# A planner's prices for TensorE products, turned blocks as plain products, and small work kept together by the array's tile size

## The chip, the core and the metric

The kernel runs on one core of a Trainium2 chip. Measured is the time of one launch on the device in microseconds (us), as the median of several runs. TensorE (PE in the profile) multiplies, VectorE (DVE), ScalarE (ACT) and GpSimd (POOL) work on rows of 128 partitions, and SyncE (SP) issues most DMA transfers. Each engine works through its own instructions in the order in which the program gives them and waits on semaphores for the others.

## What is computed

The reference is one inference step of two decoder layers in fp32 for 256 prompt rows and 8 sample rows, which share all weights. Layer 0 mixes by RWKV-7 (16 heads of 64) and S5 side by side, layer 1 by retention (8 heads, states of 256x512), and each is followed by a SwiGLU feed-forward block.

```python
for i in range(DEPTH):
    h = rmsnorm(x, norm_mix[i])
    if i % 2 == 0:
        proj = h @ w_in_a[j]                                  # 2048 x 4352
        o_rwkv, sh, S = rwkv7_mix(proj[..., :RWKV_PROJ], ...)
        o_s5, hr, hi = s5_mix(proj[..., RWKV_PROJ:], ...)
        mix = jnp.concatenate([o_rwkv, o_s5], -1) @ w_out_a[j]
    else:
        proj = h @ w_in_c[j]                                  # 2048 x 12288
        mix, S = retention_mix(proj, st_ret[j], pos, ret_gn[j], w_out_c[j])
    x = x + mix.astype(x.dtype)
    h = rmsnorm(x, norm_ffn[i])
    x = x + swiglu(h, ffn_w_gate[i], ffn_w_up[i], ffn_w_down[i]).astype(x.dtype)
```

```python
def step(S, inp):                                             # RWKV-7, one row
    r_t, w_t, k_t, v_t, kk_t, a_t = inp
    sa = jnp.einsum('bhij,bhj->bhi', S, kk_t)
    S = (S * w_t[:, :, None, :] - sa[..., None] * (kk_t * a_t)[:, :, None, :]
         + v_t[..., None] * k_t[:, :, None, :])
    return S, jnp.einsum('bhij,bhj->bhi', S, r_t)
```

## The kernel before

**The stream.** All 264 rows (256 + 8) are held transposed, and the large products run as one stream over the weights. A weight tile of 128x512 (`raw`) is split into a high part `wh` by ScalarE and a low part `wl` by VectorE, and each 128x128 block makes three matmuls with 264 columns in the type float32r: `wh` with `xh`, `wh` with `xl`, `wl` with `xh` (other names of the right-hand side are `hh`, `hl`, `n`, `omh`). So one granule of 12 stream matmuls needs one `wh` and one `wl`; `run_stream` splits two granules ahead. There are 21408 stream matmuls.

**The side work.** Everything between the large products is written as generators: `front`, `back` and `post` for the RWKV-7 heads in pairs `p` of 0 to 7 (prompt rows, in chunks of 64), `rwkv_sample` for the 8 sample rows, `s5` and `s5_out`, and in layer 1 `ret_mix` and `ret_sample`. Their operations are recorded and not issued at once. After every second k-tile, that is after every six stream matmuls, `run_stream` calls `pump`, which issues what is ready by the planner's own clocks: `clk` has one clock for each of TensorE ("P"), VectorE ("V"), ScalarE ("S"), GpSimd ("G") and the DMA ("D"), `cost` gives the price of an operation, `after` the time at which its operands are there, and `emit` moves the clock on and writes the instruction. The order so found is fixed in the program. All instructions of side work and stream are written by the same `getattr` in `emit`, so that the profile shows nearly everything as L279; the names of the tiles tell the work apart.

**Four places that matter below.** (1) `turned(out, a, one)` turns a 64x64 block by a product with `id2`, two identities of 64 below each other. It is called 8 times a pair in `front` and 22 times in `back` (8 + 6 + 8, by `heads`), for the two halves of the partitions by turns. Where the output begins at partition 0 it is a `transpose`, otherwise a plain `matmul`. (2) The S5 recurrence in `s5` has 64 steps on VectorE:

```python
for c in range(64):
    h, o = H[:, :, :, c], H[:, :, :, c + 1]
    self.mul(t, bc(h[:, None], [128, 2, 2, 32]), w)
    self.add(o, o, t[:, 0])
    self.add(o, o, t[:, 1, ::-1])
    if c % 4 == 3:
        yield
```

(3) `rwkv_sample_half` does, for each of 8 head pairs, a product with `bones` (ones in two blocks of 64), a multiply on VectorE, a subtraction on GpSimd, two DMAs which broadcast a row of `srow` into the tile `t` (in the profile `ar_tmp<-ar_tmp`), and then `self.mul(t, t, vb("k"))` on VectorE, a 128x512 multiply that needs them. (4) `ret_sample` in layer 1 updates the states of 8 sample rows a head in two groups `g` of 4: eight multiplies `stt` of 128x512 on VectorE, products with the new states on TensorE, and then `load(1)`, four DMAs of 512 KB from GpSimd's queue into the same four buffers, before the second group.

Of the kernel before, what the change touches and what calls it, by code (L numbers as in the profile page):

```python
# [10 lines left out]
F32R = mybir.dt.float32r  # L11
# [9 lines left out]
T = TP + TS  # L21
# [18 lines left out]
PART = 2, 2  # L40
LOOK = 2, 1
FAR = 1 << 20
ORDER = (("u", 0), ("u", 4), ("q", 0), ("q", 1), ("q", 2), ("q", 3))
LAG = 0.13, 0.2
PS5, PSO, PR = 0, 0, 0
# [14 lines left out]
class Task:  # L60
    def __init__(self, w, row0, nk, c0, rhs, done, need=None):
        self.w, self.row0, self.nk, self.c0 = w, row0, nk, c0
        self.rhs, self.done, self.need, self.pre = rhs, done, need, None
# [64 lines left out]
class Builder:  # L128
    def __init__(self, ctx, tc, ins, outs, dumps=None):
        self.ctx, self.tc, self.nc = ctx, tc, tc.nc  # L130
        self.I, self.O, self.C0 = ins, outs, ins["cst"]
        self.dumps = dumps or {}
        self.side, self.rec = [], None
        self.evac = Side(None, -1)
        self.clk = dict.fromkeys("PVSGD", 0.0)
        self.where, self.uses, self.pend = {}, {}, {}
        self.tick, self.cols, self.warm = 0, 0.0, False
        self.flags = Flags(self)
        self.act_set = None
        nc = self.nc  # L140
        self.V, self.G, self.S, self.P = (Eng(self, e, k) for e, k in
                                          ((nc.vector, "V"), (nc.gpsimd, "G"), (nc.scalar, "S"), (nc.tensor, "P")))
        self.Q, self.QG, self.QS = (Eng(self, e, "D") for e in (nc.sync, nc.gpsimd, nc.scalar))
        pool = lambda name, **k: ctx.enter_context(tc.tile_pool(name=name, **k))
        self.pw = pool("pw", bufs=1)
        self.pc = pool("pc", bufs=1)
        self.pb = pool("pb", bufs=1)
        self.ps = pool("ps", bufs=1, space=PSUM)
        ctx.enter_context(tc.manual_schedule())
        self.banks = [self.ps.tile([128, 512], F32, name=f"ps{i}", tag=f"ps{i}") for i in range(8)]  # L150
        self.layer, self.held = 0, {}
        self.turn, self.bank, self.open, self.busy = 0, {}, [], [None] * 4
        for b in self.banks:
            self.cells(b)


    def psum(self):
# [3 lines left out]
        self.open.append(b)  # L161
        return bass.AP(self.banks[0].tensor, self.turn * FAR, self.banks[0].ap)

    def real(self, x):

        if not hasattr(x, "ap") or not isinstance(x.offset, int) or x.offset < FAR or str(x.space) != str(PSUM):
            return x
        b = self.bank[x.offset // FAR]
        if b.at is None:
            free = [i for i in range(4) if not self.busy[i]]  # L170
            b.at = min(free, key=lambda i: self.uses[self.banks[i].tensor.name].max())
            self.busy[b.at] = b
        return bass.AP(self.banks[b.at].tensor, x.offset % FAR, x.ap)

# [25 lines left out]
    def operands(self, name, a, k):  # L200
# [3 lines left out]
        for i, x in enumerate(aps):  # L204
            if type(x.tensor).__name__ == "Tile":
                if str(x.space) == str(PSUM):
                    far = x.offset // FAR
                    out.append((far or x.tensor.name, self.cells(self.banks[0]), True))
# [4 lines left out]
    def cost(self, key, name, a):  # L213

        n = int(np.prod(a[0].shape[1:])) if hasattr(a[0], "shape") else 1
        if key == "P":
            w = a[2] if name == "transpose" else a[1]
            w = int(np.prod(w.shape[1:]))
            if a[1].dtype == F32R:
                return 0.113 * n / T  # L220
            if name == "transpose":
                return 0.11 if w > 64 else 0.04
            if w <= 32:
                return max(0.034, 0.02 + 0.42e-3 * n)
            if w <= 64:
                return max(0.08, 1.05e-3 * n)
            return max(0.205, 1.68e-3 * n)
        if key == "V":
            fast = name in ("tensor_scalar", "tensor_copy", "memset") and not any(str(x.space) == str(PSUM) for x in a if hasattr(x, "space"))
            c = 0.07 + n * (0.52e-3 if fast else 1.04e-3) + (0.006 * n if name == "reciprocal" else 0)  # L230
            if name.startswith(("tensor_scalar", "scalar")) and any(hasattr(x, "shape") and tuple(x.shape[1:]) == (1,) for x in a[2:]):
                c += 0.07
            return c
        if key == "S":
            return 0.094 + n * 0.83e-3
        if key == "D":
            return 0.03 + n * a[0].shape[0] * 1.11e-5
        return 0.035 + n * 0.83e-3 if name == "memset" else 0.15 + n * 2.05e-3

    def after(self, key, uses):  # L240

        t = 0.0
        for name, (at, bits), w in uses:
            if isinstance(name, int):
                b = self.bank[name].at
                if b is None:
                    name = min((self.banks[i].tensor.name for i in range(4) if not self.busy[i]), key=lambda n: self.uses[n].max())
                else:
                    name = self.banks[b].tensor.name
            u = self.uses[name]  # L250
            for q in (0, 1) if w else (0,):
                for e, k in enumerate("PVSG"):
                    v = u[q, e][at].max()
                    if v:
                        t = max(t, v + (LAG["P" in (k, key)] if k != key else 0.0 if key == "P" or q else 0.125))
        return t

    def emit(self, eng, name, a, k):

        a = [self.real(x) for x in a]  # L260
        key, uses = eng.key, self.operands(name, a, k)
        c = self.cost(key, name, a)
        t = self.after(key, uses)
        if key == "D":
            t = self.clk["D"] = max(t + 1.7, self.clk["D"]) + c
        else:
            if key == "P":
                while self.clk["P"] + 0.1 >= (self.tick + 1) * 3.4133:
                    self.warm = self.cols >= 3277
                    self.tick, self.cols = self.tick + 1, 0.0  # L270
                n = int(np.prod(a[0].shape[1:]))
                self.cols += n * (1 if a[1].dtype == F32R else 2 if name == "transpose" else 4) * a[1].shape[0] / 128
                c *= 1 if self.warm else 2
            elif key == "S":
                self.functions(ACT_SET.get(a[2]))
            t = self.clk[key] = max(self.clk[key], t) + c
        for n, (at, bits), w in uses:
            self.uses[n][0 if w else 1, "PVSG".index(key) if key != "D" else 3][at] = t
        getattr(eng.eng, name)(*a, **k)  # L279
        return t  # L280
# [119 lines left out]

    def turned(self, out, a, one):

        if out.offset % FAR < out.ap[0][0]:
            self.P.transpose(out, a, one)
        else:
            self.P.matmul(out, a, one, start=True, stop=True)

    def gcopy(self, out, a):
        self.G.tensor_scalar(out, a, 1.0, None, op0=OP.mult)
# [90 lines left out]
    def choices(self):  # L500

        for s in self.side + [self.evac]:
            for op in s.ops:
# [12 lines left out]
                        best = t + c, t, i  # L516
                yield best[1], s.pri, op, best[2]

    def pump(self, most):

        left = most
        while True:
            self.refill()
            now = self.clk["P"]
            other, tens = [], []
            for c in self.choices():
                if c[2].keys[c[3]] == "P":
                    if left > 0 and c[2].ready[0] <= now:
                        tens.append((c[1], c[2].ready[0], c))
                elif c[0] <= now:  # L530
                    other.append((c[0], c[1], c))
            if other:
                c = min(other, key=lambda o: o[:2])[2]
            elif tens:
                c = min(tens, key=lambda o: o[:2])[2]
            else:
                return
            t = self.clk["P"]
            self.go(c[2], c[3])
            left -= self.clk["P"] - t  # L540
# [260 lines left out]
    def in_a_tasks(self):  # L801
# [4 lines left out]
        def quad(q):  # L806
            for j in range(3):
                for e in range(2):
                    tile = 8 * j + 2 * q + e
                    n = 3 * (2 * q + e) + j  # L810
                    need = (("free",) + divmod(n - RING, 3),) if n >= RING else ("ush2",) if n >= RING - 5 else ("ush",) if n >= RING - 9 else None
                    ts.append(Task(w, 0, KT, tile * 128, rx, lambda a, t=tile: self.in_a_done(a, t), need))

        def us(t0):
            for t in range(t0, t0 + 4):
                ts.append(Task(w, 0, KT, PROJ + t * 128, rx, lambda a, t=t: self.s5_in(a, t)))

        for f, i in ORDER:
            quad(i) if f == "q" else us(i)
# [989 lines left out]
```

## Time and profile before

| | before |
|---|---|
| median of 3 runs (least, most) | 3212.47 us (3202.04, 3217.61) |
| profiled execution, its own time | 3204.68 us |
| its span | 3202.9 us |
| TensorE busy | 3121.3 us, 97% |
| VectorE busy | 1972.0 us, 62% |
| ScalarE busy | 1498.7 us, 47% |
| GpSimd busy | 343.4 us, 11% |
| DMA moved | 560.54 MB, 175 GB/s on average |

Busy time is the time in which an engine has at least one instruction under way; on TensorE successive matmuls overlap, so their single durations add up to more than that. The granted clock (PEclk) is TensorE's clock as a share of its full 2.4 GHz. In the views, `ps` is a PSUM bank, `ar_tmp`, `ar_hida`, `ar_hidb` and `ar_hidy` are large tiles out of which the side work cuts its own, `cst` holds constants (`id2`, `bones`, `ident`), and `t` with `ar_tmp` is the S5 recurrence.

### The profile page before, as it was taken

The page shows a single profiled execution, that of the slowest core. Times are in us where ns is not written, and L with a number is a line of the kernel's source. Part 1 is how long each engine was busy: PE and PEld are TensorE (multiplying, and loading weights), DVE is VectorE, ACT ScalarE, POOL GpSimd, SP SyncE. Part 2 cuts the span into 40 slices and gives each one's busy share as a digit, 9 for nine tenths or more (in the row PEclk, how much of TensorE's full clock was granted, in tenths as well). Part 3 has the DMA queues.
Part 4 walks back from the last instruction along what each step waited for, and adds up shares of the span by engine and source line. Part 5 has one row for each costly group of instructions (what it writes and reads, how often), then busy time and mean ns, then how long its engine had stood idle before and what let it go on. Part 6 is the DMA issues. An engine that isn't in the chain of part 4 may idle for free.

```text
span 3202.9 us, 65844 instructions
## 1 busy us (share of the span) xinstructions
PE 3121.3 (97%) x26390; PEld 2967.3 (93%) x26390; DVE 1972.0 (62%) x3702; ACT 1498.7 (47%) x2733; POOL 343.4 (11%) x525
## 2 busy tenths in 40 slices
PE   7999798899999999999999999999999999999998
PEld 7987687799999999999998998988899999999998
DVE  6788666466555555566566666565566565555554
ACT  6543355255444444455344444444455444444454
POOL 5111332100000000001111111011100000000001
PEclk9999899799999999999999999999999999999999
DMA  5323413455655556666666677567666555565654
GB/s 192 120 86 74 61 54 70 84 163 183 179 184 180 182 179 184 181 182 211 216 230 219 230 250 254 174 244 250 217 179 184 181 182 184 178 183 180 184 179 152
DMA packets 161138, 560.54 MB, mean 175 GB/s; under 512 B 21312, under 2 KB 23744, under 8 KB 160576
## 3 DMA queue, kind: packets, MB, share of 16 engines
q1 hardware_dynamic: 140384, 483.29, 50.7%
q0 software_dynamic: 19584, 71.31, 5.9%
q8 instruction: 207, 3.39, 0.4%
q10 hardware_dynamic: 864, 1.74, 0.1%
q14 instruction: 99, 0.81, 0.1%
HBM read 511.45 MB, written 42.69 MB: 173 GB/s over the span
## 4 chain that ended last, share of the span: by engine, by line
PE 92%; DVE 3%; DMA 2%; ACT 1%; POOL 1%; issue 0%; SPq 0%; DVEq 0%; POOLq 0%; ACTq 0%
PE ps L279 92%; DMA ar_tmp<-ar_tmp 2%; DVE ar_tmp L279 1%; POOL ar_tmp L279 1%; DVE wl L279 1%; DVE t L279 1%; ACT ar_tmp L279 0%; ACT wh L279 0%; DVE ar_hidb L279 0%; DVE ar_hidy L279 0%; SPq L279 0%; DVE xl L279 0%; DVE ar_hida L279 0%; POOL ar_hida L279 0%; ACT L285 0%
## 5 line engine op out<-in xcount | busy, mean ns | idle before, releaser
L279 DVE TENSOR_TENSOR wl<-raw,wh 128x512 fp32r<-128x512 f32 x1784 | 1260.6, 710 | 904.1 <-ACT wh L279 892.5
L279 ACT ACTIVATE wh<-raw 128x512 fp32r<-128x512 f32 x1784 | 1098.9, 628 | 936.3 <-PE ps L279 905.5
L279 PE MATMUL ps<-xh,wh 128*128 128x264 f32 x4512 | 1330.0, 295 | 14.7 <-ACT wh L279 12.4
L279 PE MATMUL ps<-xh,wl 128*128 128x264 f32 x4512 | 1289.7, 286 | 10.8 <-DVE wl L279 10.7
L279 PE MATMUL ps<-xl,wh 128*128 128x264 f32 x4512 | 1287.8, 285 | 0.0
L279 PEld LDWEIGHTS ps<-xh,wh 128*128 128x128 f32 x4512 | 858.8, 190 | 63.4 <-issue 28.6
L279 PEld LDWEIGHTS ps<-xh,wl 128*128 128x128 f32 x4512 | 856.4, 190 | 12.6 <-DVE wl L279 12.6
L279 PEld LDWEIGHTS ps<-xl,wh 128*128 128x128 f32 x4512 | 860.0, 191 | 5.7 <-issue 4.8
L279 PE MATMUL ps<-hl,wh 128*128 128x264 f32 x1280 | 364.0, 284 | 0.0
L279 PE MATMUL ps<-hh,wl 128*128 128x264 f32 x1280 | 363.9, 284 | 0.0
L279 PE MATMUL ps<-hh,wh 128*128 128x264 f32 x1280 | 363.8, 284 | 0.0
L279 PE MATMUL ps<-n,wh 128*128 128x264 f32 x1408 | 257.4, 284 | 0.0
L279 PE MATMUL ps<-ar_tmp 64*64 64x64 f32 (+8 forms) x2912 | 215.3, 283 | 39.5 <-DVE ar_tmp L279 24.6
L279 PEld LDWEIGHTS ps<-hh,wh 128*128 128x128 f32 x1280 | 241.4, 189 | 0.0
L279 PEld LDWEIGHTS ps<-hl,wh 128*128 128x128 f32 x1280 | 240.9, 188 | 0.0
L279 PEld LDWEIGHTS ps<-hh,wl 128*128 128x128 f32 x1280 | 240.7, 188 | 0.0
L279 PEld LDWEIGHTS ps<-ar_tmp 64*64 64x64 f32 (+3 forms) x2912 | 149.3, 149 | 82.3 <-DVE ar_tmp L279 28.9
L279 POOL TENSOR_TENSOR sqs<-sq,sqs 128x264 f32<-128x264 f32 x56 | 42.4, 758 | 1663.5 <-ACT sq L279 1663.5
L279 PEld LDWEIGHTS ps<-n,wh 128*128 128x128 f32 x1408 | 217.8, 188 | 0.0
L279 PE MATMUL ps<-n,wl 128*128 128x264 f32 x704 | 199.6, 284 | 0.0
L279 PE MATMUL ps<-omh,wh 128*128 128x264 f32 x512 | 147.1, 287 | 0.0
L279 PE MATMUL ps<-omh,wl 128*128 128x264 f32 x512 | 145.6, 284 | 0.0
(214 smaller groups left out, 2872.1 us busy)
## 6 DMA issues: line engine op xcount, KB each, us to landing
raw<-in_w_in_c_dram SPq DMA_DIRECT2D x192, 512.0 KB, 4.3
raw<-in_ffn_w_gate_dram SPq DMA_DIRECT2D x176, 512.0 KB, 3.6
raw<-in_ffn_w_up_dram SPq DMA_DIRECT2D x176, 512.0 KB, 3.7
raw<-in_ffn_w_down_dram SPq DMA_DIRECT2D x176, 512.0 KB, 3.7
out_dram<-ar_tmp POOLq DMA_DIRECT2D x72, 512.0 KB, 4.3
raw<-in_w_in_a_dram SPq DMA_DIRECT2D x68, 512.0 KB, 3.7
ar_tmp<-in_state_ret_dram POOLq DMA_DIRECT2D x64, 512.0 KB, 6.9
raw<-in_w_out_c_dram SPq DMA_DIRECT2D x64, 512.0 KB, 3.8
```

The lines of the kernel that those rows point to most:

```text
L279: getattr(eng.eng, name)(*a, **k)
```

## The change

It has four parts. `cost` prices a product by its weight load (0.004 us and 0.833 ns a column) or its columns, whichever is more, and twice that for fp32. `turned` always writes a plain `matmul`. A new function `tile_of` gives the tile size of the array that a product needs (32, 64 or 128 rows and columns; float32r and transposes count as 128 columns) and its place, and `emit` keeps a clock for each place: products of one size at different places run side by side, and a change of size waits for all and costs 0.09 us and a load more. In `pump`, of the products with the same priority those of the array's present size go first; if all that are ready have another size, `pump` returns, until the oldest has been ready for 2.5 us (`PATIENCE`) or they come to 1.2 us of cost (`TOGETHER`).

```diff
+PATIENCE = 2.5, 2.5
+TOGETHER = 1.2, 1.2
...
@@ cost
+            load = 0.004 + 0.833e-3 * w
             if a[1].dtype == F32R:
-                return 0.113 * n / T
+                return max(load, 0.005 + 0.44e-3 * n)
             if name == "transpose":
-                return 0.11 if w > 64 else 0.04
-            if w <= 32:
-                return max(0.034, 0.02 + 0.42e-3 * n)
-            if w <= 64:
-                return max(0.08, 1.05e-3 * n)
-            return max(0.205, 1.68e-3 * n)
+                return max(load, 0.42e-3 * n)
+            return 2 * max(load, 0.002 + 0.833e-3 * n)
...
+    def tile_of(self, name, a):
+
+        r = lambda n: 32 if n <= 32 else 64 if n <= 64 else 128
+        w = a[1]
+        m = 128 if name == "transpose" or w.dtype == F32R else r(int(np.prod(w.shape[1:])))
+        size = r(int(w.shape[0])), m
+        return size, (w.offset // w.ap[0][0], a[0].offset % FAR // a[0].ap[0][0])
...
@@ emit
                 c *= 1 if self.warm else 2
+                size, at = self.tile_of(name, a)
+                t0 = max(self.clk["P"], t)
+                if size != self.size:
+                    t0 = max([t0, *self.tiles.values()]) + 0.09 + 0.833e-3 * size[1]
+                    self.size, self.tiles = size, {}
+                t0 = max(t0, self.tiles.get(at, 0.0))
+                t = self.tiles[at] = t0 + c
+                self.clk["P"] = t if size == (128, 128) else t0 + 0.012
             elif key == "S":
                 self.functions(ACT_SET.get(a[2]))
-            t = self.clk[key] = max(self.clk[key], t) + c
+            if key != "P":
+                t = self.clk[key] = max(self.clk[key], t) + c
...
     def turned(self, out, a, one):
 
-        if out.offset % FAR < out.ap[0][0]:
-            self.P.transpose(out, a, one)
-        else:
-            self.P.matmul(out, a, one, start=True, stop=True)
+        self.P.matmul(out, a, one, start=True, stop=True)
...
@@ pump
                 if c[2].keys[c[3]] == "P":
                     if left > 0 and c[2].ready[0] <= now:
-                        tens.append((c[1], c[2].ready[0], c))
+                        tens.append((c[1], self.size_of(c[2]) != self.size, c[2].ready[0], c))
...
             elif tens:
-                c = min(tens, key=lambda o: o[:2])[2]
+                if not went and all(o[1] for o in tens) and now - min(o[2] for o in tens) < PATIENCE[self.layer]:
+                    if sum(self.cost("P", *x[1:3]) for o in tens for x in o[3][2].calls[0]) < TOGETHER[self.layer]:
+                        return
+                c = min(tens, key=lambda o: o[:3])[3]
+                went = True
```

Since the planner's clocks differ, the whole order of the side work in the stream differs. Two places on VectorE show it. The first is in the part of layer 0 in which the S5 recurrence runs (`t_77<-t_77,ar_tmp` are its adds, `ar_tmp<-t_77,ar_tmp` its multiply, `wl` the split that the stream needs next, the other rows belong to `front` and `back` of the head pairs). Before, eight successive rows there were:

```order
L279 TENSOR_TENSOR wl<-raw,wh 128x512
L279 TENSOR_TENSOR t_77<-t_77,ar_tmp 128x64
L279 TENSOR_TENSOR ar_hidb<-ar_hidy,ar_hida 64x4x64
L279 TENSOR_TENSOR t_77<-t_77,ar_tmp 128x64
L279 TENSOR_TENSOR ar_tmp<-ar_tmp,ps_70 128x256
L279 TENSOR_TENSOR wl<-raw,wh 128x512
L279 TENSOR_TENSOR ar_tmp<-t_77,ar_tmp 128x128
L279 TENSOR_TENSOR ar_tmp<-ps_71,cst 128x256
```

With the change, a stretch between two `wl` in the same part reads (shown without its last rows):

```order
L296 TENSOR_TENSOR wl<-raw,wh 128x512
L296 TENSOR_TENSOR ar_tmp<-t_77,ar_tmp 128x128
L296 TENSOR_TENSOR ar_tmp<-ps_70,cst 128x256
L296 TENSOR_TENSOR t_77<-t_77,ar_tmp 128x64 x2
L296 TENSOR_TENSOR ar_tmp<-t_77,ar_tmp 128x128
L296 TENSOR_TENSOR t_77<-t_77,ar_tmp 128x64
L296 SCALAR_TENSOR_TENSOR ar_tmp<-ps_69,cst 128x256
L296 TENSOR_TENSOR t_77<-t_77,ar_tmp 128x64
L296 TENSOR_TENSOR ar_tmp<-t_77,ar_tmp 128x128
L296 TENSOR_TENSOR ar_tmp<-ps_71,cst 128x256
L296 TENSOR_TENSOR t_77<-t_77,ar_tmp 128x64 x2
L296 TENSOR_TENSOR ar_tmp<-t_77,ar_tmp 128x128
```

Five steps of the recurrence now stand between two `wl` here (two more adds, one more multiply and one more add follow until the next `wl`), where two adds stand between the two `wl` of the rows before.

The second place is in `ret_sample` of layer 1, at the border between the two groups of states of the first head (`SCALAR_TENSOR_TENSOR ar_tmp<-ar_tmp,ps_..` are the state multiplies; behind the last one of the first group, the second such row of each piece, the four buffers are loaded anew). Before:

```order
L279 SCALAR_TENSOR_TENSOR ar_tmp<-ar_tmp,ps_69 128x512
L279 TENSOR_TENSOR wl<-raw,wh 128x512
L279 SCALAR_TENSOR_TENSOR ar_tmp<-ar_tmp,ps_70 128x512
L279 TENSOR_TENSOR wl<-raw,wh 128x512 x6
L279 TENSOR_TENSOR ar_tmp<-ps_75,rstd 128x264
L279 TENSOR_TENSOR wl<-raw,wh 128x512
L279 TENSOR_TENSOR ar_tmp<-ps_76,rstd 128x264
L279 SCALAR_TENSOR_TENSOR ar_tmp<-ar_tmp,ps_71 128x512
```

With the change:

```order
L296 SCALAR_TENSOR_TENSOR ar_tmp<-ar_tmp,ps_71 128x512
L296 SCALAR_TENSOR_TENSOR ar_tmp<-ar_tmp,ps_72 128x512
L296 TENSOR_TENSOR wl<-raw,wh 128x512 x4
L296 SCALAR_TENSOR_TENSOR ar_tmp<-ar_tmp,ps_69 128x512
L296 SCALAR_TENSOR_TENSOR ar_tmp<-ar_tmp,ps_70 128x512
```

Four `wl` instead of seven stand between the last state multiply of the first group and the first of the second, and the multiplies come in twos.

## Rows read from the trace of the kernel before

**Rows 1.** The page: busy time of each engine, and granted clock in 40 slices.
```profile
PE 3121.3 (97%) x26390; PEld 2967.3 (93%) x26390; DVE 1972.0 (62%) x3702; ACT 1498.7 (47%) x2733; POOL 343.4 (11%) x525
PEclk9999899799999999999999999999999999999999
```
**Rows 2.** Stretches: us, busy PE, PEld, DVE, ACT, POOL, then clock, DMA share, GB/s.
```profile
300.00:400.00 100.00, 79.30 (x789) 64.92 (x789) 61.54 (x147) 28.75 (x81) 35.08 (x55) 0.80 0.43 62
500.00:600.00 100.00, 81.46 (x898) 66.09 (x896) 58.59 (x136) 33.66 (x69) 21.07 (x24) 0.84 0.42 69
700.00:1400.00 700.00, 699.83 (x5770) 699.56 (x5769) 410.37 (x700) 338.23 (x598) 8.67 (x12) 1.00 0.60 182
```
**Rows 3.** What TensorE waited for: us in total, times, longest.
```profile
PE ps L279 <- DVE ar_tmp L279: 28.6, 13, 7.3
PE ps L279 <- ACT wh L279: 12.4, 2, 8.6
PE ps L279 <- DVE wl L279: 10.7, 6, 3.9
```
**Rows 4.** What VectorE waited for in the first 700 us.
```profile
DVE ar_tmp L279 <- DMA ar_tmp<-ar_tmp: 50.0, 8, 9.1
```
**Rows 5.** Timeline of VectorE, a multiply after its broadcast: start, us, instruction, [idle before].
```profile
303.18 0.69 DVE L279 TENSOR_TENSOR ar_tmp<-ar_tmp 128x512 f32<-128x512 f32 x1 [5.95 <-DMA ar_tmp<-ar_tmp]
303.79 0.27 DVE L279 TENSOR_TENSOR t<-t,ar_tmp 128x64 f32<-128x64 f32 x1
303.97 0.41 DVE L279 TENSOR_TENSOR ar_tmp<-ar_tmp,ps 128x256 f32<-128x256 f32 x1
```
**Rows 6.** Timeline of TensorE behind that multiply.
```profile
304.43 1.12 PE L279 MATMUL ps<-ar_tmp 64*64 64x64 f32 x16 [5.19 <-DVE ar_tmp L279]
```
**Rows 7.** Timeline of TensorE: groups of 64x64 products between stream matmuls.
```profile
235.32 1.15 PE L279 MATMUL ps<-ar_tmp 64*64 64x64 f32 x32
...
364.23 0.68 PE L279 MATMUL ps<-ar_tmp 64*64 64x64 f32 x16
...
479.49 1.78 PE L279 MATMUL ps<-cst,ar_tmp 64*64 64x64 f32 x12
```
**Rows 8.** Groups of TensorE instructions by shape, the turned blocks: busy us, mean ns, idle before.
```profile
L279 PE MATMUL ps<-cst,ar_tmp 64*64 64x64 f32 x192 | 30.6, 256 | 0.1
...
L279 PE MATMUL ps<-cst,ar_hida 64*64 64x64 f32 x75 | 11.3, 243 | 0.0
...
L279 PE MATMUL ps<-cst,ar_hidb 64*64 64x64 f32 x45 | 7.4, 260 | 1.3 <-DVE ar_tmp L279 1.3
...
L279 PE MATMUL ps<-cst,t 64*64 64x64 f32 x48 | 7.1, 243 | 0.0
```
**Rows 9.** Groups of VectorE instructions by shape, 100 to 700 us.
```profile
L279 DVE TENSOR_TENSOR wl<-raw,wh 128x512 fp32r<-128x512 f32 x150 | 113.0, 757 | 41.5 <-ACT wh L279 40.5
L279 DVE TENSOR_TENSOR t<-t,ar_tmp 128x64 f32<-128x64 f32 x128 | 40.3, 315 | 1.2
L279 DVE TENSOR_TENSOR ar_tmp<-ar_tmp,ps 128x256 f32<-128x256 f32 x72 | 29.3, 414 | 11.2 <-PE ps L279 10.6
L279 DVE TENSOR_TENSOR ar_tmp<-t,ar_tmp 128x128 f32<-128x128 f32 x64 | 27.1, 424 | 0.5
```
**Rows 10.** Timelines of TensorE, GpSimd and VectorE in layer 1, a reload of states.
```profile
1578.33 0.39 PE L279 MATMUL ps<-xh,wh 128*128 128x264 f32 x1
...
1578.67 1.58 POOL L279 DMA_DIRECT2D ar_tmp<-in_state_ret_dram  x3 [2.01 <-PE ps L279]
...
1588.47 0.69 DVE L279 SCALAR_TENSOR_TENSOR ar_tmp<-ar_tmp,ps 128x512 f32<-128x512 f32 x1 [1.43 <-PE ps L279]
```
**Rows 11.** The tile of the retention states: its 64 loads, from issue to landing.
```profile
DMA to landing us min/median/max: 3.8/6.9/12.5
```
**Rows 12.** Two stretches with turned blocks, columns as in the stretches above.
```profile
192.00:199.00 7.00, 7.00 (x49) 5.10 (x48) 5.03 (x13) 2.74 (x6) 3.18 (x7) 0.74 0.05 4
482.00:485.40 3.40, 3.40 (x36) 2.92 (x34) 2.24 (x6) 2.87 (x4) 1.35 (x4) 0.51 0.73 246
```

More of the change, by code (lines that the diff above doesn't have):

```diff
@@ L137, in __init__ @@
         self.tick, self.cols, self.warm = 0, 0.0, False
+        self.size, self.tiles = None, {}
         self.flags = Flags(self)
@@ L517, in choices, with size_of @@
                 yield best[1], s.pri, op, best[2]
+    def size_of(self, op):
+        return self.tile_of(*op.calls[0][0][1:3])[0]
     def pump(self, most):
-        left = most
+        left, went = most, False
         while True:
```

## The prediction

> **What bounds the kernel now.** I read the page first. TensorE is busy 97% of the span, mostly at the full clock level [rows 1]: it sets the time, so a microsecond counts only if TensorE works less, waits less or runs at the higher clock for longer. The view of stretches shows where anything is left to win. From 700 us on, TensorE does 5770 stream matmuls in 699.83 us, 0.1213 us each, at granted clock 1.00; before that, slices of 100 us fall to 79.30 and 81.46 us busy at clocks of 0.80 and 0.84 [rows 2]. Layer 0's small work lies there. The waits of TensorE name what is late: VectorE's `ar_tmp` above all, 28.6 us in 13 waits, then ScalarE's `wh` and VectorE's `wl` [rows 3]. Largely they go back to one thing: VectorE sits idle 50.0 us, eight times, until a DMA has brought the broadcast row of the sample state [rows 4]. Its multiply at 303.18 stood 5.95 us for that [rows 5], and TensorE's next product 5.19 us behind it [rows 6].
>
> **The turned blocks.** `turned` is called 240 times (8 head pairs of 8 in `front` and 22 in `back`); 120 were transposes, by turns with plain products. A plain fp32 product is two rows in the trace, a transpose one. A group of 12 rows (4 transposes, 4 products) takes 1.78 us, a group of 8 plain products (16 rows) 0.68 us [rows 7]: 1.10 less per 8, and 30 eights make 33. Check from the other side: all 360 rows of this kind are busy 30.6 + 11.3 + 7.4 + 7.1 = 56.4 us [rows 8]; 30 x 0.68 is 20.4, so 36 less. I take 33 and keep 36 as the bound. The other bound: if such a block gained only by a shared switch, 0. The rows leave no doubt that the alternation is what costs, since 16 rows are shorter than 12.
>
> The Trainium skill has a sentence the other way: "TensorE: Matmul & The Clock Gate", section Terms, says of the weight load and the matmul that their transpose mode is four times faster for FP32. By that the 120 turned blocks would lose: a plain one is 0.68 / 8 = 0.085 us [rows 7], a quarter of that 0.021, and 120 x 0.064 would be 7.7 us more. The trace does not agree in this setting.
>
> **The list by tile size.** It should merge groups of small products. Counted through both orders, it hardly does: changes of tile size other than those of the transposes go from 555 to 540, and the groups of small work between stream matmuls from 159 to 172 in layer 0 (155 to 163 in layer 1). Two eights in one group take 1.15 us, two apart 2 x 0.68 [rows 7], so a merge of two is worth 0.21 and saves two switches: 0.1 each. Fifteen switches are 1.5 to 2 us. TensorE's own work becomes 33 + 2 = **35 us** less.
>
> **What moves with the prices.** Small work is put earlier, and all of it comes from the planner's clocks, which do not know three things.
>
> *The broadcast.* The planner's DMA price is unchanged, so the eight multiplies still stand too early on VectorE. What lies on TensorE between the `bones` product ahead of a broadcast and the first product that needs the multiply is the cover. In the new order it is thinner over the eight: 42 stream matmuls fewer (222 to 180) and 49 switches fewer (121 to 72, those of 23 turned transposes among them). 42 x 0.1213 = 5.1; 49 at 0.1 to 0.14 (1.10 us over 8 switches of a group [rows 7]) make 5 to 7. A thinner cover is a longer wait: **+12**; nothing if other work is late as well, and with the rest of the cover's products 17.
>
> *The S5 recurrence.* Its 64 steps on VectorE (a 128x128 multiply and two 128x64 adds) stand between stream matmuls 768 and 1338 before, and between 752 and 1082 after; the rows of the order above show five steps between two `wl` where the piece of before has two adds. In the densest part, 108 stream matmuls from the 972nd, stand 42 steps, 10 `wl` and some 42 operations 256 wide. VectorE: a step is 27.1 / 64 + 2 x 40.3 / 128 = 1.05, so 44.2; `wl` 10 x 113.0 / 150 = 7.5; 42 x 29.3 / 72 = 17.1 [rows 9]: 69 us. TensorE has 108 x 0.1213 = 13.1 there, 35 eights at 1.15 - 0.68 = 0.47, 16.5, for 18 groups twice 0.1 and some 4 of others: 37 us. VectorE works in order, and `wl` behind the steps is what the stream needs. Rows on VectorE overlap: a 0.69 starts the next after 0.61, a 0.27 after 0.18 [rows 5]. With 0.085 off each of these 178 rows, 69 becomes 54. So TensorE waits 17 to 32 us in this part, where some 5 of the `wl` waits stood before [rows 3]: **+15**, near the lower end since what lies beside the part can take some of the steps (10 to 27).
>
> *The states of layer 1.* In the second order the first state multiply after a reload stands 30 stream matmuls behind the resumed stream, not 78. The load goes out at 1578.67, 0.34 us after the stream resumes at 1578.33, and the multiply starts at 1588.47 [rows 10]. Landings take 3.8, 6.9 and 12.5 us (least, median, most) [rows 11]. Thirty stream matmuls are 3.6 us, so VectorE waits about 3 us at the median; the next product that hangs on it comes near 9 us, so TensorE waits 0 to 1 at the median and up to 4 at the longest, eight times: **+3** (0 to 30).
>
> *The clock.* A stretch with turned blocks at 192 to 199 stands at 0.74 of the full clock, one at 482 to 485.4 at 0.51, without a wait before them [rows 12]; half clock is the 1.2 GHz level. The transposes that fill them go, and I give back **-5**. New waits can bring other half-clock stretches (+5), all of them gone would be -15.
>
> **The sum.** -35 + 15 + 12 + 3 - 5 = -10. The profiled execution took 3204.68 us, so 3195; it is 0.24% under the median of 3212.47, and against that the sum is 3202. By the bounds: -36 + 10 + 0 + 0 - 15 = -41, and -33 + 27 + 17 + 30 + 5 = +46. Less than 0.5%, 16 us, is about what a measurement of this kernel can't tell from no change.
>
> **The rivals.** *The gain stays.* VectorE's backlog in the recurrence and the broadcasts is absorbed, because the stream's look-ahead of two granules covers 24 matmuls (2.9 us) each time and waits for the broadcast also shorten when TensorE comes earlier to the `bones` product. For it: TensorE was late for VectorE for only 28.6 + 10.7 us in 19 waits [rows 3], and VectorE is busy 62% of the span [rows 1]. Against it: the densest part has nearly twice as much VectorE as TensorE work. Sum: -35 + 0 + 3 + 0 - 5 = -37, so 3175.
>
> *Slower: no overlap in the dense part.* The 42 steps stand in line with the 256-wide operations which the head pairs' products need in turn. If each of the 18 groups waits for VectorE, and VectorE for the group, the part takes VectorE's 69 and 18 x 1.15 of products, 90, not 37: +53 for +15, so 3240. It decides from about 79 us on for these 108 stream matmuls: 42 over the 37, so +17 in the sum. For it: the first product after a broadcast waits like this [rows 6]. Against it: two chains of head pairs run side by side, so one's products lie under the other's VectorE work.
>
> *It does not do what it says.* The list merges little; that is in the forecast already, at 2 us. *Transposes are the cheaper form*: +8 for -33, so 3243; the group rows speak flatly against it, 0.02. The Trainium skill's sentence on FP32 above is of this kind.
>
> **How the numbers follow.** Forecast (gain mostly eaten, 3186 to 3220): 0.50. The gain stays (3165 to 3190): 0.30. No overlap (3225 to 3255): 0.18. Dear products: 0.02. Under 3196 lie the second and a little of the first, 0.33; over 3228 the third, most of it, and the last, 0.19; between, 0.48. The range from 3170 to 3228 leaves out the far end of the second and the slower cases.
>
> **What would show it.** Turned groups of 16 rows in 0.6 to 0.7 us, and busy time of these rows near 20 us. VectorE's idle time for the broadcast's DMA at 50 to 62 us. In the stretch of the recurrence, VectorE over 90% busy and TensorE waiting for `wl` and `ar_tmp` 15 us more than before. In layer 1 VectorE waits for `in_state_ret_dram`, TensorE hardly. If TensorE waits no more than before in the recurrence, the second case holds; if that part takes 80 us, the third. Wrong in another way would be a change in layer 0's half-clock time by over 15 us.

## The result, and the profile after

The changed kernel takes 3259.47 us (median of 4 runs, 3258.57 to 3264.98) against 3211.47 of the kernel before in the same comparison: ratio 1.0156, 95% interval 1.0128 to 1.0183. It is 48 us slower, outside the predicted range.

The page of the profiled execution, busy time and granted clock:

```profile
span 3258.2 us, 66180 instructions
...
PE 3107.4 (95%) x26510; PEld 2957.4 (91%) x26510; DVE 1980.2 (61%) x3685; ACT 1504.8 (46%) x2752; POOL 341.6 (10%) x525
...
PEclk9998799789999999999999999999999999999999
```

Read it against the span, not by itself: TensorE is busy 13.9 us less than in [rows 1], and idle 3258.2 - 3107.4 = 150.8 us where it was idle 3202.9 - 3121.3 = 81.6. So 69.2 us of new waiting stand against the gain. The waits of TensorE name VectorE most of all, 70.8 us in 36 waits for 28.6 in 13 [rows 3]:

```profile
PE ps L296 <- DVE ar_tmp L296: 70.8, 36, 8.4
PE ps L296 <- ACT wh L296: 15.2, 7, 8.6
PE ps L296 <- ACT ar_tmp L296: 9.5, 2, 9.1
PE ps L296 <- DVE wl L296: 8.2, 11, 1.9
```

The turned blocks did what was said. Their groups by shape, those of [rows 8], are now:

```profile
L296 PE MATMUL ps<-cst,ar_tmp 64*64 64x64 f32 x256 | 11.0, 223 | 3.7 <-DVE ar_tmp L296 3.7
L296 PE MATMUL ps<-cst,ar_hida 64*64 64x64 f32 x100 | 5.3, 255 | 0.9 <-DVE ar_hida L296 0.9
L296 PE MATMUL ps<-cst,ar_hidb 64*64 64x64 f32 x60 | 3.2, 245 | 0.0
L296 PE MATMUL ps<-cst,t 64*64 64x64 f32 x64 | 2.7, 224 | 0.4 <-DVE t L296 0.4
```

480 rows in 22.2 us of busy time for 360 rows in 56.4: 34.2 less. All of TensorE's work fell by only 13.9, since other work took longer, in part at a lower clock: up to the 2400th stream matmul the mean granted clock is 0.92 before and 0.90 after.

Where the time went is seen at equal places of the stream. Counted through the records, the 2400th stream matmul, behind all small work of layer 0, starts at 708.5 us before and at 743.5 after: +35. From the 8800th to the 16000th, which hold the side work of layer 1, it is 1048.9 before and 1069.2 after: +20. Stretches of after (the first holds the dense part of the recurrence) and of before (the part with the same stream matmuls, and layer 1):

```profile
200.00:262.00 62.00, 46.60 (x712) 40.01 (x710) 59.44 (x185) 13.50 (x29) 6.14 (x11) 0.83 0.17 48
300.00:400.00 100.00, 65.69 (x655) 54.05 (x653) 51.44 (x124) 29.43 (x84) 34.47 (x51) 0.78 0.45 54
1400.00:2400.00 1000.00, 987.29 (x7515) 907.47 (x7514) 603.09 (x995) 447.10 (x761) 132.94 (x193) 1.00 0.66 218
```
```profile
190.00:227.00 37.00, 37.00 (x367) 31.21 (x365) 30.00 (x82) 14.71 (x29) 8.46 (x15) 0.91 0.22 72
1400.00:2400.00 1000.00, 1000.00 (x7681) 924.11 (x7680) 616.82 (x1021) 458.37 (x782) 137.86 (x199) 1.00 0.67 221
```

In the dense part VectorE works 59.44 of 62 us and TensorE 46.60, where before TensorE did not stand still; in layer 1 TensorE, which never stood still there either, is idle 12.7 us. The other 7.6 of the 20 us are longer work, of which two short stretches at half clock explain 3.4. What TensorE waited for in the dense part (196 to 260 us):

```profile
PE ps L296 <- DVE ar_tmp L296: 8.5, 5, 2.2
PE ps L296 <- ACT ar_hidy L296: 4.2, 1, 4.2
PE ps L296 <- DVE ar_hidb L296: 3.1, 2, 1.9
PE ps L296 <- POOL ar_hida L296: 0.7, 1, 0.7
```

No `wl` is among them: the stream itself did not wait, the small products of the head pairs did. What VectorE waited for, first in layer 0, as in [rows 4], then in layer 1:

```profile
DVE ar_tmp L296 <- DMA ar_tmp<-ar_tmp: 61.0, 8, 9.6
```
```profile
DVE ar_tmp L296 <- DMA ar_tmp<-in_state_ret_dram: 15.2, 9, 3.1
```

In layer 1 VectorE waits for the reloaded states as predicted, but TensorE's waits are elsewhere: eight for VectorE and two long ones for GpSimd.

```profile
PE ps L296 <- DVE ar_tmp L296: 7.3, 8, 1.5
PE ps L296 <- POOL t L296: 4.6, 2, 2.4
```

The timelines of GpSimd, VectorE and TensorE show one of the eight, the rotary of a head of `ret_mix` ahead of its first product:

```profile
1751.32 1.65 POOL L296 TENSOR_TENSOR ar_tmp<-ar_tmp 128x528 f32<-128x528 f32 x1 [10.92 <-DVE ar_tmp L296]
...
1753.00 0.71 DVE L296 TENSOR_TENSOR ar_tmp<-ar_tmp 128x528 f32<-128x528 f32 x1 [1.23 <-POOL ar_tmp L296]
1753.63 0.68 DVE L296 TENSOR_TENSOR wl<-raw,wh 128x512 fp32r<-128x512 f32 x1
1754.23 0.70 DVE L296 TENSOR_TENSOR ar_tmp<-ar_tmp 128x528 f32<-128x528 f32 x1
...
1754.99 1.57 PE L296 MATMUL ps<-ar_hidy,ar_tmp 128*128 128x256 f32 x8 [1.44 <-DVE ar_tmp L296]
```

GpSimd's row, VectorE's two and the `wl` between them follow each other, and TensorE reaches the product 1.44 us too early. Something has moved the product ahead of the work that it needs, and there are eight such waits in layer 1, which has eight heads. That is not the price of a row on GpSimd or VectorE, which this change leaves alone.

**The theories.** A: the new clock of `emit` itself runs too fast in groups. Products of one size at different places should run side by side in it, but `after` returns the end of the last write into the same PSUM bank, TensorE's own writes included, and all places of a group write into one bank. So they are charged in series. The states' products of layer 1 are the plainest case: eight products with 512 columns on tiles of 128x32 are 8 x 2 x (0.002 + 0.833e-3 x 512) = 6.9 us in the clock, and on the chip:

```profile
1612.12 1.92 PE L296 MATMUL ps<-ar_tmp 128*32 128x512 f32 x16
```

The old price was 8 x (0.02 + 0.42e-3 x 512) = 1.9. Five microseconds of stream that aren't there, twice a head, are 41 stream matmuls each, about the 48 by which the state multiply came closer to its reload. Rivals: B, no order would keep the gain, since TensorE then waits longer for the broadcasts; C, the list by tile size holds products back; D, the old clock's lag behind the chip was slack that covered other engines' low prices.

### The profile page after: what moved, and what is told of

Same layout as the page of the kernel before. It is cut to its first block, busy times and chain, and to the rows that moved or that the text cites. A ratio compares the mean times of both kernels' runs of the same rounds, so it can differ in the third digit from the quotient of the medians.

```text
span 3258.2 us, 66180 instructions
## 1 busy us (share of the span) xinstructions
PE 3107.4 (95%) x26510; PEld 2957.4 (91%) x26510; DVE 1980.2 (61%) x3685; ACT 1504.8 (46%) x2752; POOL 341.6 (10%) x525
## 4 chain that ended last, share of the span: by engine, by line
PE 84%; DVE 6%; DMA 3%; ACT 3%; POOL 2%; issue 2%; SPq 0%; DVEq 0%; POOLq 0%; ACTq 0%
PE ps L296 84%; DVE ar_tmp L296 3%; DMA ar_tmp<-ar_tmp 3%; DVE wl L296 1%; POOL ar_tmp L296 1%; DVE t L296 1%; ACT ar_tmp L296 1%; ACT wh L296 1%; DVE ar_hida L296 0%; ACT t L296 0%; DVE xl L296 0%; ACT L302 0%; ACT ar_hidy L296 0%; DVE ar_hidb L296 0%; DMA out_dram<-ar_tmp 0%
## 5 line engine op out<-in xcount | busy, mean ns | idle before, releaser
L296 PEld LDWEIGHTS ps<-xh,wh 128*128 128x128 f32 x4512 | 859.0, 190 | 71.1 <-ACT wh L296 30.1
L296 PE MATMUL ps<-ar_tmp 64*64 64x64 f32 (+6 forms) x2912 | 219.8, 287 | 46.6 <-DVE ar_tmp L296 25.5
L296 PEld LDWEIGHTS ps<-ar_tmp 64*64 64x64 f32 (+2 forms) x2912 | 153.1, 152 | 90.1 <-issue 31.8
```

## The experiments

Medians against the kernel before, measured in turn with it (its medians were 3211.47 us beside the changed kernel, and 3207.0, 3215.15, 3217.19 and 3209.53 in the four groups of runs that followed, so differences of some 10 us between groups are not clear of noise). "Own writes" and "broadcast" are the two corrections of the planner below.

| run | prices, clock | blocks | list | corrections | us | ratio, 95% interval |
|---|---|---|---|---|---|---|
| changed kernel | new | plain | yes | | 3259.47 | 1.0156 (1.0128 to 1.0183) |
| e1_turned_only | old | plain | no | | 3178.56 | 0.990 (0.9871 to 0.9929) |
| e2_own_writes | new | plain | yes | own writes | 3206.31 | 0.999 (0.9972 to 1.0008) |
| e4_no_list | new | plain | no | | 3259.36 | 1.0152 (1.0122 to 1.0182) |
| e7_order_transposed | new | as before | yes | | 3273.27 | 1.0199 (1.0163 to 1.0235) |
| e5_stream_price | new, stream old | plain | yes | own writes | 3207.08 | 0.9978 (0.9962 to 0.9994) |
| e9_engine_prices | new, DVE and POOL dearer | plain | yes | own writes | 3204.09 | 0.9984 (0.9967 to 1.0001) |
| e6_broadcast_price | new | plain | yes | both | 3147.39 | 0.9804 (0.9773 to 0.9834) |
| e8_turned_broadcast | old | plain | no | broadcast | 3116.88 | 0.9708 (0.9672 to 0.9743) |
| e12_broadcast_only | new | plain | yes | broadcast | 3212.70 | 0.9994 (0.9982 to 1.0006) |
| e15_before_broadcast | old | as before | no | broadcast | 3174.35 | 0.9873 (0.9835 to 0.9911) |
| e10_budget | new, budget | plain | yes | both | 3135.84 | 0.9755 (0.9729 to 0.9782) |
| e11_list_old_clock | old | plain | yes | broadcast | 3148.93 | 0.9798 (0.9775 to 0.982) |
| e13_no_list_both | new | plain | no | both | 3160.08 | 0.984 (0.9814 to 0.9866) |
| e14_no_list_budget | new, budget | plain | no | both | 3170.32 | 0.9871 (0.9845 to 0.9897) |

**The blocks alone, in either order.** e1 is the kernel before with the diff of `turned` and nothing else:

```diff
-        if out.offset % FAR < out.ap[0][0]:
-            self.P.transpose(out, a, one)
-        else:
-            self.P.matmul(out, a, one, start=True, stop=True)
+        self.P.matmul(out, a, one, start=True, stop=True)
```

> The kernel before with one part of the change: every turned block is a plain product; prices, planner's clock and list as before. Theory A (the blocks are worth what the rows say, and the loss comes from the order that the new prices make): the order stays nearly that of before, so 33 to 37 us less, about 3177 (3168 to 3188). Rival B (TensorE, being quicker, only waits longer for the broadcasts and VectorE, so that no order would keep the gain): 3195 to 3212. If the blocks gain nothing: 3212.

3178.56, 28 us less (23 to 41 by the interval): Theory A's number; B is out, since the gain is there as soon as the order is left alone. e7 is the changed kernel with its 120 transposes put back when the instruction is written, behind all planning:

```diff
+        if name == "matmul" and a[2].tensor.name == self.cst.tensor.name and tuple(a[2].shape) == (64, 64) and a[0].offset % FAR < a[0].ap[0][0]:
+            name, k = "transpose", {}
         getattr(eng.eng, name)(*a, **k)
```

> The changed kernel in its own order, instruction for instruction, only that the 120 blocks with an output at partition 0 are written as transposes again at the very end. It prices the blocks alone. If the term of 33 to 36 us holds in this order: 3290 to 3300. If the waits of the new order hide much of it: 3262 to 3285. By the rule that a transpose is the cheaper form: 3250.

3273.27, only 14 more, as the second case had it. Its page shows why:

```profile
span 3270.8 us, 65940 instructions
...
PE 3144.0 (96%) x26390; PEld 2979.4 (91%) x26390; DVE 1980.5 (61%) x3685; ACT 1509.8 (46%) x2752; POOL 342.5 (10%) x525
```

TensorE is busy 36.6 us more than in the changed kernel, and idle 126.8 us for 150.8. Two thirds of the work taken out there had been replaced by waiting: in an order whose products stand ahead of what they need, quicker products mostly wait longer.

**The list.** e4 is the changed kernel with the size taken out of the order of `tens`, and without waiting for company:

```diff
-                        tens.append((c[1], self.size_of(c[2]) != self.size, c[2].ready[0], c))
+                        tens.append((c[1], not True and self.size_of(c[2]) != self.size, c[2].ready[0], c))
...
-                if not went and all(...
+                if not True and not went and all(...
```

> The changed kernel without the list by tile size: products go by priority and readiness as before, nothing waits for company; prices, clock and plain blocks stay. Theory A: the planner's clock is what it was, so the loss stays in both layers: 3250 to 3280. Rival C: the loss goes: 3175 to 3210.

3259.36 against 3259.47: the list is not what costs the changed kernel its 48 us, and C is out as their cause. It does merge: without it the groups of small work in layer 0 are 187 for 171, and the changes of tile size 576 for 540. In the two profiles TensorE works 4.6 us less with the list and is idle 3.2 us more, so that little is left in the time.

**The planner's own writes.** e2 is the changed kernel with two lines in `after`:

```diff
                 for e, k in enumerate("PVSG"):
+                    if k == key == "P":
+                        continue
                     v = u[q, e][at].max()
```

> The changed kernel, but the planner no longer lets a product wait for TensorE's own earlier writes into the same PSUM bank (the clock of each place keeps them in order). Theory A: since all places of a group write into one bank, the changed planner charges products that run side by side one after another; a group of 16 rows 128x32 with 512 columns takes 1.92 us on the chip and near 7 in its clock. So it believes the other engines to be done too early. With this taken away the waits that are new in layer 1, some 20 us, go, and a good part of those new in layer 0: 3175 to 3215, about 3195. Rival C (the list holds products back until the work of other engines comes too late): the list is still there, so 3245 to 3265.

3206.31, 53 us less, within A's range and far from C's. The page, and TensorE's waits in layer 1, which shrink to one row, none longer than half a microsecond:

```profile
span 3202.7 us, 66149 instructions
...
PE 3078.1 (96%) x26510; PEld 2937.3 (92%) x26510; DVE 1976.0 (62%) x3681; ACT 1511.5 (47%) x2756; POOL 351.3 (11%) x525
```
```profile
PE ps L298 <- DVE ar_tmp L298: 5.3, 14, 0.5
```

By equal places the 2400th stream matmul starts at 698.7 and the 8800th to the 16000th take 1058.4: 45 us come from layer 0 and 11 from layer 1, of its 20. Of the 55.5 us of span, 26.2 are idle time of TensorE and 29.3 its work, with the granted clock up to the 2400th stream matmul back at 0.93.

Two places show that it is the mechanism of A. In all eight heads of layer 1, 78 stream matmuls start between the last products of the first group of states and the first state multiply of the second, exactly as before (33 to 48 in the changed kernel), and VectorE no longer waits for the reload at all. And the 108 stream matmuls of the recurrence's dense part now take 30.1 us with 2.9 us of waiting, where the changed kernel has 64 with 16.5, since the side work is spread again: 89 rows of VectorE stand there for 191. Put into the changed kernel with the broadcast price below, the same two lines gain 65 us (e12 to e6). The groups of small work in layer 0 fall from 171 to 146 and changes of tile size from 540 to 486, a larger merging than the list's own.

What A does not explain: e2 has the plain blocks and still lies 28 us above e1, with TensorE idle for 124.6 us.

**Slack and prices of other engines.** e5 and e9 add to e2, the one the old price of a stream matmul, the other dearer rows on VectorE and GpSimd:

```diff
-                return max(load, 0.005 + 0.44e-3 * n)
+                return 0.113 * n / T
```
```diff
-            c = 0.07 + n * (0.52e-3 if fast else 1.04e-3) + ...
+            c = 0.13 + n * (0.52e-3 if fast else 1.04e-3) + ...
...
-        return 0.035 + n * 0.83e-3 if name == "memset" else 0.15 + n * 2.05e-3
+        return 0.035 + n * 0.83e-3 if name == "memset" else 0.15 + n * 3.2e-3
```

> As the run that took the wait for TensorE's own writes out of the planner (3206.31 us), and the stream matmul priced as in the kernel before, 0.113 instead of 0.121 us. Theory D (the old prices left the planner's clock far behind the chip, and this slack is what covered the other engines' low prices): waits of TensorE fall, 3180 to 3195. If that slack did nothing: 3203 to 3210.

> As the run that took the wait for TensorE's own writes out of the planner (3206.31 us), with VectorE's price up by 0.06 us an instruction and GpSimd's from 2.05 to 3.2 ns a column (the 128x528 row took 1.85 us on the chip and is priced at 1.23). If the waits outside the broadcasts come from these low prices: 15 to 25 us less, 3180 to 3192. If they come from the thin cover alone: 3200 to 3212.

3207.08 and 3204.09: neither moves it beyond the noise. Theory D falls in this form, and so does the explanation by VectorE's and GpSimd's prices.

**The broadcasts.** The first of the three things that the prediction named. A DMA from tile to tile is priced at 7.0 us, the median from issue to landing of the broadcasts in the kernel before (the last number):

```profile
ar_tmp<-ar_tmp SPq DMA_DIRECT2D x16, 128.0 KB, 7.0
```

```diff
-            t = self.clk["D"] = max(t + 1.7, self.clk["D"]) + c
+            far = all(type(x.tensor).__name__ == "Tile" for x in a[:2])
+            t = self.clk["D"] = max(t + (7.0 if far else 1.7), self.clk["D"]) + c
```

It was put into four kernels: e6 (on e2), e8 (on e1), e12 (on the changed kernel) and e15 (on the kernel before).

> As the run that took the wait for TensorE's own writes out of the planner (3206.31 us), and a DMA from one on-chip tile to another, the broadcasts above all, priced at 7.0 us instead of 1.7. If the eight broadcast waits come from that price: VectorE's idle time for them, 57.2 us there, falls under 15, TensorE gets back 30 to 45: 3160 to 3180. If the multiply is then only placed later and something else waits in its place: 3190 to 3210.

> The kernel before with plain turned blocks (3178.56 us alone) and the same price of 7.0 us for a DMA from tile to tile. If the broadcast waits come from that price: 30 to 40 us less, 3135 to 3150. If another wait takes their place: 3165 to 3180.

> The changed kernel with the broadcast price of 7.0 us alone, the wait for TensorE's own writes left in. If the two corrections act on different waits (53 us for the own writes, 59 for the broadcasts): about 3200. If the broadcast waits are what the own writes made longer: 3150 to 3165. If the broadcasts can't be gained while the clock runs fast: 3235 to 3260.

> The kernel before with the broadcast price of 7.0 us alone; turned blocks half transposes as before. If the broadcast waits and the blocks are worth the same apart and together (plain blocks 28 to 30 us alone, and 62 us between the two runs with plain blocks): 3145 to 3155. If the price only pays with plain blocks: 3175 to 3205.

It takes away 59, 62, 47 and 35 us (e15 against the kernel before in its own group of runs). e6 and e8 gained more than was expected; e12, at 3212.70, lies between two of its cases, nearest to that of separate waits; e15, at 3174.35, is at the lower edge of the case that the price pays only with plain blocks. Apart, blocks and price are worth 28 and 35 us, together (kernel before to e8) some 95: about 30 more than their sum; why is open.

For e1 and then e8: the page, what VectorE waited for in layer 0, and the stretch up to 700 us:

```profile
span 3176.7 us, 66100 instructions
...
PE 3084.1 (97%) x26510; PEld 2943.1 (93%) x26510; DVE 1968.0 (62%) x3701; ACT 1501.3 (47%) x2734; POOL 343.6 (11%) x525
```
```profile
DVE ar_tmp L279 <- DMA ar_tmp<-ar_tmp: 49.3, 8, 7.8
```
```profile
0.00:700.00 700.00, 620.01 (x6764) 556.02 (x6764) 501.24 (x1236) 333.01 (x707) 183.73 (x298) 0.93 0.42 105
```
```profile
span 3114.7 us, 66110 instructions
...
PE 3058.0 (98%) x26510; PEld 2923.8 (94%) x26510; DVE 1962.8 (63%) x3695; ACT 1503.5 (48%) x2742; POOL 344.1 (11%) x525
```
```profile
DVE ar_tmp L280 <- DMA ar_tmp<-ar_tmp: 4.8, 3, 3.1
```
```profile
0.00:700.00 700.00, 655.60 (x7269) 598.10 (x7270) 535.70 (x1296) 370.72 (x775) 187.53 (x301) 0.98 0.44 121
```

VectorE's wait falls by 44.5 us. TensorE's idle time falls from 92.6 to 56.7 us, and its busy time, for the same 26510 rows, by 26.1: the granted clock up to 700 us rises from 0.93 to 0.98. That the clock falls around these waits can be seen at the last broadcast of e1: TensorE's first product behind it, and the stretch around it, at half clock.

```profile
599.35 0.48 PE L279 MATMUL ps<-ar_tmp,ar_hida 64*64 64x64 f32 x4 [6.28 <-DVE ar_tmp L279]
```
```profile
597.00:614.00 17.00, 14.65 (x133) 12.50 (x134) 5.81 (x17) 1.32 (x3) 2.32 (x5) 0.50 0.29 86
```

Such a wait costs itself and a slower clock around it. e8 is faster than both kernels.

**What is left.** With both corrections the new prices (e6, 3147.39) still lose 30 us to the old ones (e8, 3116.88). e10 charges small products to the budget of a call, e11 puts the list onto e8, e13 and e14 take it from e6 and e10 by e4's diff:

```diff
-            left -= self.clk["P"] - t
+            left -= max(self.clk["P"] - t, 0.08 * len(c[2].calls[0]) if c[2].keys == "P" else 0.0)
```
```diff
+                self.size = self.tile_of(name, a)[0]
...
-                c = min(tens, key=lambda o: o[:2])[2]
+                if not went and all(o[1] for o in tens) and now - min(o[2] for o in tens) < PATIENCE[self.layer]:
+                    if sum(self.cost("P", *x[1:3]) for o in tens for x in o[3][2].calls[0]) < TOGETHER[self.layer]:
+                        return
+                c = min(tens, key=lambda o: o[:3])[3]
+                went = True
```

> As the run with both corrections of the planner (own writes and broadcast price, 3147.39 us), but a product is charged at least 0.08 us against the budget of a call of the pump; with the new clock it was charged 0.012. Against 3116.88 us of the old prices with plain blocks and the broadcast price, 30 us are still missing. If they come from that budget (groups of 32 products and more, which drain the chains ahead of VectorE): 3118 to 3132. If from the prices themselves: 3142 to 3152.

> The kernel before with plain turned blocks and the broadcast price (3116.88 us), and the change's list by tile size and its waiting for company on top, with the old prices and the old clock. Groups fall from 161 to 143 in layer 0 and changes of size from 549 to 480. By 0.1 to 0.14 us a change, if nothing else moves: 7 to 10 less, 3107 to 3110. If what is held back comes too late for other engines: 3120 to 3150.

> The changed kernel with both corrections of the planner (3147.39 us), without the list by tile size and with the change's own charge of the budget. If the list costs: 3115 to 3135. If it does nothing: 3143 to 3152.

> The changed kernel with both corrections of the planner and the charge of 0.08 us a product (3135.84 us), and without the list by tile size. If holding back is what costs there too, as it cost 32 us with the old clock: 3105 to 3122. If the list pays once groups are priced rightly: 3140 to 3155. If it does nothing, as in the changed kernel alone: 3132 to 3140.

The budget gives 12 us (3135.84, between its two cases), not clear of the noise between groups. The list costs 32 on e8 (3148.93, the case that what is held back comes too late), gains 13 on e6 (3160.08 without it, outside both cases) and 34 on e10 (3170.32 without it, outside all three), and does nothing in the changed kernel; the 13 are not clear of noise. That one rule acts with both signs suggests that a shift of the order by itself moves this kernel by some 30 us; no run shows that directly. A's 53 and 65 us lie above it. Where the last 19 to 30 us of the new prices go was not found.

## Why the prediction was wrong

- **The sum in two parts.** TensorE's work was to fall by 40 us (35, and 5 by the clock) and its waits to grow by 30 (15 + 12 + 3). The pages have 13.9 and 69.2.
- **The turned blocks, 33 to 36 less: right.** 34.2 by their rows; as a time 28 in the old order (3207.0 to 3178.56), 14 in the new one. By the estimate that the prediction made from the sentence of the Trainium skill ("TensorE: Matmul & The Clock Gate", Terms) on a four times faster transpose mode for FP32, they would have lost 7.7. No run here agrees with it.
- **The list, 2 us: right in effect**, nothing measurable without it (e4). That it hardly merges was read from a count in which list and new clock act together; by itself it takes away 36 changes of tile size.
- **The broadcasts, +12: right in kind, a little small.** VectorE's idle time went from 50.0 to 61.0 us. On TensorE the first waits behind the eight multiplies add up to 37.8 us before and 55.7 after, +18.
- **The recurrence, +15: the size by luck.** TensorE is idle for 16.5 of the 64 us that the part takes, where it did not wait before. But the 5 us of `wl` waits that the prediction took off did not stand in this part, and the waits are not the stream's for `wl` but those of the head pairs' products. Besides the 37 us of work as counted, some 10 are half clock (0.85 on average), which no term had here. The rival without overlap had 90 us for the part and isn't what happened.
- **The states of layer 1, +3 (0 to 30): mis-sized, and in another place.** VectorE does wait for the reloads, 15.2 us. TensorE lost 20, of which 12.7 are waits, at the rotary and behind GpSimd's queue, which the term didn't look at.
- **The clock, -5: wrong in sign.** The blocks alone do raise it (0.92 to 0.93 up to the 2400th stream matmul, e1). In the changed kernel new waits brought new half-clock stretches, and it fell to 0.90.
- **The step that failed** is "all of it comes from the planner's clocks, which do not know three things". They did not know a fourth, and it was new with the change: products that run side by side in one bank were charged in series, so that the clock ran fast in groups and side work was placed too early. Each of the three places was costed by itself; of the 69.2 us of new idle time, 18 are at the broadcasts, 16 in the recurrence, 13 in layer 1, and some 22 in short waits elsewhere in layer 0, for which there was no term. With the fourth taken away (e2) TensorE's work is 43.2 us less than before and its idle time 43.0 more, nearer to the 40 and 30 of the forecast, though not place by place. The 78 stream matmuls that became 30 stood in the prediction, and 48 x 0.1213 = 5.8 us was about the size of that error for one group, read as a fact about one load and not as a clock that runs fast in every group.

## What to carry to other kernels

Where a planner's prices set the order, hold its price of one whole group against the group's row in the trace: prices meant for single products can be wrong by a factor of more than three for eight that overlap (6.9 us for 1.92), through a dependence rule that another function adds. A part of a change that is worth its rows (here the plain blocks) is best tried in the old order first, and a wait that every version shows (here the broadcasts) is worth pricing before work is made shorter. Where one rule moves the time by 30 us with either sign, one run with it and one without say nothing about the rule in general; what tells is a second pair in another order, and the place in the trace where the mechanism must show (here the 78 stream matmuls that come back).

## What the runs showed of the hardware that was not expected

Removing 44.5 us of VectorE's waits for a DMA gave back 62 us of span: on TensorE 35.9 us of idle time and 26.1 us of busy time, with the granted clock up from 0.93 to 0.98 over the first 700 us. And 36.6 us of TensorE work, put back in the same order, cost 12.6 us of span, since 24.0 us of its waits went.
